# Feed-forward tail: running sums held on the chip, the residual added by the output's DMA, a quarter of two convolutions on ACT and POOL, and the second up weights split earlier

## The chip, the cores and the metric

The kernel runs on one core of a Trainium2 chip. The metric is the device time of one execution in microseconds (us). TensorE (PE) does matmuls, VectorE (DVE), ScalarE (ACT) and GpSimd (POOL) work element by element, and SyncE (SP) and POOL issue DMAs.

## The reference

One block of a diffusion model, depth 1, on 2048 tokens of width 1024, in float32. What matters here is its second half:

```python
h_lat = h_lat + mod_l[2] * rmsnorm(mix_l, g_post_mix[l])          # residual after the token mix
hl = modulate(h_lat, g_pre_ffn[l], mod_l[3], mod_l[4])
z = (hl @ w_up).reshape(1, 32, 64, 5632)                          # up projection, tokens as a 32 x 64 grid
z = depthwise_conv_3x3(z, conv_w) + conv_b
f_l = (gelu(z[..., :2816]) * z[..., 2816:]) @ w_down              # down projection
h_lat = h_lat + mod_l[5] * rmsnorm(f_l, g_post_ffn[l])
```

The first half (normalisation, a recurrent unit, pooling, a gated unit, an output projection) makes `mix_l` and is not touched, apart from where its result is kept.

## The kernel before, in words

Every float32 operand of a large matmul is split into two float16 halves, and each product is three matmuls (high by high, high by low, low by high). `hT` (128 x 2 x 8 x 2048 float16, 64 KB in each partition) holds the split input of the up projection for all tokens.

The feed-forward part goes over 22 chunks `c` of 128 channels, each with a pair `ab` (the gelu side and the product side). For a chunk, `up` (L835) does 8 blocks of 24 matmuls of 128 x 512 into the two "B" banks, and ACT copies each block into `z`. `conv` (L986) does the 3 x 3 convolution of the chunk in two halves `q` of 16 rows and two sides: ACT writes the middle tap into a PSUM tile, and DVE adds the eight others with one instruction each (L1002); then comes gelu, the product (L1010) and a sum of squares for the scale of the split. Two chunks make a group, eleven groups in all. `split_g` (L1014) splits a group's products, and `down` (L1030) multiplies them with the down weights, in 16 tiles `t` of 128 tokens, 12 matmuls each. The 16 sums over groups live in device memory as `accd`: the first group writes them, later ones add to them with an accumulating DMA that POOL issues (L1064, tile `dd`). The last group instead loads `accd` back (L1040), loads the residual `hlat` (L1042), and `finish` (L1067) adds, normalises and writes the output.

The weights of a chunk are loaded and split by `load_up` (L815): a scale from the sum of squares (ACT L151, one small matmul `sct`, DVE), the high half on ACT (L825), a scaled copy on ACT (L827), the low half on POOL (L828). Chunk 0 is prepared while the output projection of the token mix runs (`i == 5` in the loop over its 16 tiles), chunk 1 in the first pass of the chunk loop. That loop (from L1080) lets `up` of chunk c, `conv` of chunk c-1 and `down` of the group before advance by turns; a scheduler with a timeline of its own then sets the order of each engine's instructions, which run in order on the chip. Work on the last group's two halves, and what is left of group 9 (12 of its 16 tiles), comes after the last up projection. That stretch is called the tail.

Of the kernel before, what the change touches and what calls it, by code (L numbers as in the profile page):

```python
# [15 lines left out]
D = 1024  # L16
# [52 lines left out]
def block_kernel(ctx: ExitStack, tc: tile.TileContext, x, xT, ctx_d, ctxT, cc, crow, cols_d, wm01, bm01, wmT,  # L69
# [32 lines left out]

    hlat = dram.tile([L, D], F32, name="hlat")
    ybc = [dram.tile([128, 4, CH], F32, name=f"ybc{n}") for n in range(NCH)]
# [77 lines left out]
    def rawt(name):  # L182
        return wspp.tile([128, 1024], F32, tag="raw", bufs=2, name=name)

# [630 lines left out]
    def load_up(c):  # L815

        r = fwc.tile([128, 2, 1024], F32, tag="ur", bufs=1, name="ur")
        S.dma_start(r, wup[c].rearrange("p a k m -> p a (k m)"))
        w = (fwc if c % 2 == 0 else ff).tile([128, 2, 2, 1024], F16, tag="uw", bufs=1, name="uw")

        def steps():
            stat(w[:, 0].bitcast(BF16), [r], upsc[:, c, :])
            V.tensor_scalar(upinv[:, c:c + 1], upsc[:, c, 1:2], sc_f[:, 1:2], None, op0=OP.mult)
            yield
            A.activation(w[:, 0], r, AF.Copy, scale=upsc[:, c, 0:1])  # L825
            yield
            A.activation(r, r, AF.Copy, scale=upsc[:, c, 0:1])  # L827
            G.tensor_tensor(w[:, 1], r, w[:, 0], op=OP.subtract)  # L828
            yield

        return w.rearrange("p h a (k m) -> p h a k m", k=KT), steps()

# [3 lines left out]
    def up(c, z, w, order=(0, 1, 2, 3)):  # L836
        for b in order:
            for ab in range(2):
                ps = pB("up")
                mm3(ps, lambda k: w[:, 0, ab, k, :], lambda k: w[:, 1, ab, k, :],  # L840
                    lambda k: hT[:, 0, k, b * CH:(b + 1) * CH], lambda k: hT[:, 1, k, b * CH:(b + 1) * CH])
# [4 lines left out]
    yscale = {}  # L846

# [33 lines left out]
    def residual(n, tt, ps, xr):  # L881
# [45 lines left out]
    for i in range(len(tiles) + 2):  # L927
        if i < len(tiles):
            n, tt = tiles[i]
            if tt == 2 and OUT.index(n) + 2 < NCH:  # L930
                y_scale(OUT[OUT.index(n) + 2])
            pr[i] = project(n, tt)
        if i == 5:
            wn, lu = load_up(0)
            list(lu)
        if 0 <= i - 1 < len(tiles):
            residual(*tiles[i - 1], *pr[i - 1])
        if i == len(tiles):
            z0 = zp.tile([128, 2, 32, 64], F32, tag="z", name="z")
            up0 = up(0, z0, wn, OUT)  # L940
# [42 lines left out]

    def conv(c, z, gs, gsq):

        for q in range(2):  # L986
            r0 = q * 16
            cv = []
            for ab in range(2):
                def wt(dy, dx):  # L990
                    return col("fcw", (c + NP * ab) * 9 + (dy + 1) * 3 + dx + 1)
# [39 lines left out]
    def down(gi, q, sp, di):  # L1031
# [35 lines left out]
    def finish(t, a, hr):  # L1067
# [12 lines left out]
    dws, queue = {}, []  # L1080
    dn, cvn, ld = nothing, nothing, nothing
    gs, gsq = None, None
    for c in range(NP + 1):
        gi, i = divmod(c, GRP)
        if c < NP:
            z = (ff if c % 2 else zp).tile([128, 2, 32, 64], F32, tag="z", bufs=1, name="z") if c else z0
            upn, lu = up(c, z, wn) if c else nothing, nothing
            if c + 1 < NP:
                wn, lu = load_up(c + 1)
            if i == 0:  # L1090
                ld = load_down(gi)
        else:
            upn = lu = nothing
        for s in range(8):
            next(upn, None)
            if s > 0:
                next(lu, None)
                if s % 2 == 0:
                    next(ld, None)
            if c != NP - 1:  # L1100
                for _ in range(1 if c < NP else 2):
                    if next(dn, queue) is queue and queue:
                        dn = queue.pop(0)
                        next(dn)
            next(cvn, None)
            if s % 4 == 3 and c > 0 and i == 0:
                q = s // 4
                queue.append(down(gi - 1, q, *split_g(gi - 1, q, gs, gsq)))
        if 2 <= c < 10:
# [4 lines left out]
        if c < NP:  # L1114
            if i == 0:
                gs = [[], []]
                gsq = small.tile([128, 2, GRP], F32, tag="gsq", bufs=2, name="gsq")
            cvn = conv(c, z, gs, [gsq[:, q, i:i + 1] for q in range(2)])
    for d in [dn] + queue:
# [96 lines left out]
```

## Time and profile before

| | us |
|---|---|
| median of 3 runs (2192.57 to 2199.12) | 2194.92 |
| the profiled execution | 2195.05 |
| its span, first to last instruction | 2193.3 |
| PE busy | 2034.2 (93%) |
| DVE busy | 1593.0 (73%) |
| ACT busy | 1192.5 (54%) |
| POOL busy | 603.0 (27%) |

The slices of the page show three stretches in which PE is far from full after the start: around 400 to 560 us (inside the token mix), around 780 us (between chunk 0 and chunk 1 of the feed-forward part), and from about 2095 us to the end. A busy PE is not PE at full speed: the granted clock (PEclk, 1.00 is 2.4 GHz and 0.50 is 1.2 GHz) is to be read with it.

### The profile page before, as it was taken

How to read it: one execution, taken by the hardware profiler on the slowest of the kernel's cores; microseconds unless marked ns; L12 is line 12 of the kernel's file. 1: busy time of each engine (PE TensorE's matmuls, PEld its weight loads, DVE VectorE, ACT ScalarE, POOL GpSimd, SP SyncE). 2: the span in 40 equal slices, each digit the busy share in tenths (PEclk: the TensorE clock that was granted, in tenths of full speed). 3: DMA queues.
4: the chain of work that ended last, by engine and by line, in shares of the span. 5: the costliest groups of instructions: out<-in, count | busy, mean ns of one | idle time of the engine just before them, and what ended most of it. 6: DMA issues, size and time to landing. Idle time of an engine off the chain costs nothing.

```text
span 2193.3 us, 24364 instructions
## 1 busy us (share of the span) xinstructions
PE 2034.2 (93%) x9215; PEld 935.4 (43%) x9215; DVE 1593.0 (73%) x2218; ACT 1192.5 (54%) x1661; POOL 603.0 (27%) x453
## 2 busy tenths in 40 slices
PE   6868989797999979999999999999999999999964
PEld 1433444343455434444444444444444444444421
DVE  5687788999554279867787677668776776778844
ACT  4676755454354456656565555646465555645431
POOL 2232334444255321002121211211122221212144
PEclk8889999898999989999999999999999999999987
DMA  7521153513332110325455554545454454444387
GB/s 292 191 93 60 66 161 110 157 37 104 130 135 100 69 58 29 135 87 108 81 124 88 124 91 83 106 68 105 87 106 87 87 106 87 88 86 87 64 236 256
DMA packets 77514, 239.48 MB, mean 109 GB/s; under 512 B 7890, under 2 KB 18514, under 8 KB 72530
## 3 DMA queue, kind: packets, MB, share of 16 engines
q1 hardware_dynamic: 56660, 162.42, 22.0%
q0 software_dynamic: 20736, 75.51, 21.2%
q8 instruction: 72, 1.18, 0.2%
q14 instruction: 46, 0.38, 0.1%
HBM read 128.84 MB, written 109.05 MB: 108 GB/s over the span
## 4 chain that ended last, share of the span: by engine, by line
PE 69%; DVE 13%; DMA 6%; issue 5%; ACT 5%; POOL 2%; SPq 0%; POOLq 0%; DVEq 0%; ACTq 0%
PE up L359 13%; PE up L361 13%; PE up L360 13%; PE dn L1049 6%; PE dn L1051 6%; PE dn L1050 6%; PE wo L874 3%; PE wo L876 3%; PE wo L878 3%; DVE wm L660 2%; DMA ac<-accd 1%; DMA wm<-in_wmT_dram 1%; DVE lru L479 1%; ACT L136 1%; DMA hT<-in_wm_dram 1%
## 5 line engine op out<-in xcount | busy, mean ns | idle before, releaser
L1002 DVE SCALAR_TENSOR_TENSOR cv<-z,cols,cv 128x1008 f32<-128x1008 f32 (+2 forms) x704 | 871.6, 1251 | 278.7 <-ACT cv L995 186.6
L359 PE MATMUL up<-hT,uw 128*128 128x512 f16 x1408 | 535.3, 380 | 6.2 <-ACT uw L825 3.7
L361 PE MATMUL up<-hT,uw 128*128 128x512 f16 x1408 | 534.7, 380 | 6.3 <-POOL uw L828 6.3
L360 PE MATMUL up<-hT,uw 128*128 128x512 f16 x1408 | 535.1, 380 | 0.0
L1064 POOL DMA_DIRECT2D accd<-dd x144 | 124.6, 865 | 762.4 <-ACT dd L1060 756.3
L842 ACT ACTIVATE z<-up,upinv 128x512 f32<-128x512 f32 x176 | 120.8, 686 | 355.3 <-PE up L361 354.8
L1049 PE MATMUL dn<-dw,gs 128*128 128x512 f16 x704 | 270.8, 385 | 33.3 <-DVE ac L1055 30.4
L1060 ACT ACTIVATE dd<-dn,gdi 128x512 f32<-128x512 f32 x320 | 214.1, 680 | 115.9 <-PE dn L1051 111.2
L1050 PE MATMUL dn<-dw,gs 128*128 128x512 f16 x704 | 271.1, 385 | 0.0
L1051 PE MATMUL dn<-dw,gs 128*128 128x512 f16 x704 | 269.9, 386 | 0.0
L361 PEld LDWEIGHTS <-uw 128*128 128x128 f16 x1408 | 137.9, 98 | 174.1 <-POOL uw L828 7.2
L359 PEld LDWEIGHTS <-uw 128*128 128x128 f16 x1408 | 139.0, 99 | 168.8 <-ACT uw L825 3.8
L360 PEld LDWEIGHTS <-uw 128*128 128x128 f16 x1408 | 138.0, 98 | 168.2 <-issue 4.7
L828 POOL TENSOR_TENSOR uw<-ur,uw 128x2048 f16<-128x2048 f32 x22 | 89.5, 4068 | 196.8 <-ACT ur L827 165.2
L136 ACT ACT_TABLE_LOAD x77 | 98.8, 1283 | 47.9 <-PE rp L443 24.1
L1050 PEld LDWEIGHTS <-gs 128*128 128x128 f16 x704 | 69.5, 99 | 117.7 <-issue 43.3
L1049 PEld LDWEIGHTS <-gs 128*128 128x128 f16 x704 | 72.9, 104 | 81.2 <-issue 4.9
L995 ACT ACTIVATE cv<-z,cols 128x1024 f32<-128x1024 f32 x88 | 106.0, 1205 | 2.0
L1051 PEld LDWEIGHTS <-gs 128*128 128x128 f16 x704 | 69.6, 99 | 85.8 <-issue 4.6
L979 POOL TENSOR_TENSOR dw<-dr,dw 128x1024 f16<-128x1024 f32 x22 | 46.4, 2125 | 117.3 <-PE dn L1051 100.6
L874 PE MATMUL wo<-wo,ysp 128*128 128x512 f16 x256 | 77.2, 383 | 1.1 <-ACT gm L807 1.1
L876 PE MATMUL wo<-wo,ysp 128*128 128x512 f16 x256 | 77.2, 383 | 0.0
(299 smaller groups left out, 3013.5 us busy)
## 6 DMA issues: line engine op xcount, KB each, us to landing
accd<-dd POOLq DMA_DIRECT2D x144, 512.0 KB, 5.3
ur<-in_wup_dram SPq DMA_DIRECT2D x22, 1024.0 KB, 5.6
wm<-in_wmT_dram SPq DMA_DIRECT2D x64, 256.0 KB, 2.9
dr<-in_wdn_dram SPq DMA_DIRECT2D x22, 512.0 KB, 4.4
hT<-in_wm_dram SPq DMA_DIRECT2D x8, 1024.0 KB, 14.5
xt<-in_xT_dram SPq DMA_DIRECT2D x8, 1024.0 KB, 7.0
ro<-in_wout_dram SPq DMA_DIRECT2D x16, 512.0 KB, 4.0
xr<-in_x_dram SPq DMA_DIRECT2D x16, 512.0 KB, 3.5
```

Source lines behind the costliest of these rows:

```text
L359: T.matmul(ps, wh(k), hh(k), start=(k == 0), stop=False)
L360: T.matmul(ps, wh(k), hl(k), start=False, stop=False)
L361: T.matmul(ps, wl(k), hh(k), start=False, stop=(k == KT - 1))
L842: A.activation(z[:, ab, b * 8:(b + 1) * 8, :], ps.rearrange("p (r x) -> p r x", x=64), AF.Identity, scale=upinv[:, c:c + 1])
L874: T.matmul(ps[h], ysp[:, 0, k, :], wk[:, 0, h * CH:(h + 1) * CH], start=st, stop=False)
L876: T.matmul(ps[h], ysp[:, 0, k, :], wk[:, 1, h * CH:(h + 1) * CH], start=False, stop=False)
L1002: V.scalar_tensor_tensor(o, z[:, ab, ya + dy:yb + dy, xa + dx:xb + dx], wt(dy, dx), o, op0=OP.mult, op1=OP.add)
L1049: T.matmul(ps[h], hi, wh, start=i == 0, stop=False)
L1050: T.matmul(ps[h], hi, wl, start=False, stop=False)
L1051: T.matmul(ps[h], lo, wh, start=False, stop=i == n - 1)
L1060: A.activation(d[:, h * CH:(h + 1) * CH], ps[h], AF.Copy, scale=di)
L1064: G.dma_start(accd[t], d, accum_op=OP.add)
```

## The change

Five edits. (1) `load_up(1)` moves from the chunk loop to `i == 9` of the output projection's loop, and the loads of later chunks follow. For odd chunks the split weights go to two tiles of a pool `rwp` that is kept to the end. (2) The residual goes into the output tensor instead of `hlat`, and `finish` adds the normalised sum to it with an accumulating DMA issued by POOL. (3) After the last up projection `hT` is not read any more; the 16 sums are loaded from `accd` into its memory (`acc`), the 12 tiles of group 9 that come in the tail are added there by POOL, and the last group adds to it on DVE. (4) In chunks 20 and 21, the product side of the second half of the convolution is done by ACT (a scaled copy per tap) and POOL (an addition per tap). (5) In the tail, odd tiles use the "B" banks, and in `finish` every fourth tile is scaled on ACT and POOL instead of DVE.

```diff
+            w = [rwp.tile([128, 2, 1024], F16, tag="raw", name=f"uw{e}") for e in range(2)]
...
-        S.dma_start(hlat[tok:tok + 128, :], hl)
+        kept[tok // 128] = S.dma_start(out[tok:tok + 128, :], hl)
...
+        if i == 9:
+            wn, lu = load_up(1)
+            list(lu)
...
+    def conv_pool(c, z, cvp):
+
+        t = fwc.tile([128, 2, 16, 64], F32, tag="uw", bufs=1, name="cvp")
+        cvp.append(t[:, 0])
+        m = fwc.tile([128, 2, 16, 64], F32, tag="ur", bufs=1, name="tap")
+        w = [col("fcw", (c + NP) * 9 + e) for e in range(9)]
+        A.activation(t[:, 0], z[:, 1, 16:32, :], AF.Identity, bias=col("fcb", c + NP), scale=w[4])
+        yield
+        for n, (dy, dx) in enumerate(TAPS):
+            ya, yb, xa, xb = area(16, dy, dx)
+            o, v = (e[:, ya - 16:yb - 16, xa:xb] for e in (t[:, 0], m[:, n % 2] if n % 3 else t[:, 1]))
+            A.activation(v, z[:, 1, ya + dy:yb + dy, xa + dx:xb + dx], AF.Copy, scale=w[(dy + 1) * 3 + dx + 1])
+            G.tensor_tensor(o, o, v, op=OP.add)
+            yield
...
-            if last:
-                a = fa.tile([128, D], F32, tag="dd", bufs=3, name="ac")
-                S.dma_start(a, accd[t])
-                hr = ff.tile([128, D], F32, tag="dr", name="hr")
-                S.dma_start(hr, hlat[t * 128:(t + 1) * 128, :])
-            ps = [pC(f"dn{h}") for h in range(2)]
+            tail = phase["tail"]
+            ps = [(pB if tail and t % 2 else pC)(f"dn{h}") for h in range(2)]
...
-                    b = a[:, h * CH:(h + 1) * CH]
+                    b = acc[:, t, h * CH:(h + 1) * CH]
                     V.scalar_tensor_tensor(b, ps[h], di, b, op0=OP.mult, op1=OP.add)
-                finish(t, a, hr)
+                finish(t, acc[:, t, :])
...
+                elif tail:
+                    G.tensor_tensor(acc[:, t, :], acc[:, t, :], d, op=OP.add)
                 else:
                     G.dma_start(accd[t], d, accum_op=OP.add)
...
+    acc = hT.bitcast(F32).rearrange("p a k t -> p (a k t)").rearrange("p (t d) -> p t d", d=D)
...
-        V.scalar_tensor_tensor(a, a, m[:, 1:2], gm5, op0=OP.mult, op1=OP.mult)
-        G.tensor_tensor(hr, a, hr, op=OP.add)
-        S.dma_start(out[t * 128:(t + 1) * 128, :], hr)
+        if t % 4 == 3:
+            A.activation(a, a, AF.Copy, scale=m[:, 1:2])
+            G.tensor_tensor(a, a, gm5, op=OP.mult)
+        else:
+            V.scalar_tensor_tensor(a, a, m[:, 1:2], gm5, op0=OP.mult, op1=OP.mult)
+        end = G.dma_start(out[t * 128:(t + 1) * 128, :], a, accum_op=OP.add)
...
+            phase["tail"] = True
+            for t in range(NT):
+                S.dma_start(acc[:, t, :], accd[t])
```

The order of the instructions moves at three places that matter. The first is ACT's row at the end of chunk 0's up projection. `uw` and `ur` are split and raw up weights (of chunk 1 before, of chunk 2 now), `dw` and `dr` the same for the down weights, `cv` the middle taps of the first convolution. Before:

```order
L842 ACTIVATE z<-up,upinv 128x512
L151 ACTIVATE uw,stt<-ur 128x2048
L151 ACTIVATE dw,stt<-dr 128x1024 x2
L842 ACTIVATE z<-up,upinv 128x512 x3
L995 ACTIVATE cv_5800<-z,cols 128x1024
L995 ACTIVATE cv_5877<-z,cols 128x1024
L825 ACTIVATE uw<-ur,upsc 128x2048
```

Now:

```order
L846 ACTIVATE z<-up,upinv 128x512
L150 ACTIVATE dw,stt<-dr 128x1024 x2
L846 ACTIVATE z<-up,upinv 128x512 x3
L150 ACTIVATE uw,stt<-ur 128x2048
L1025 ACTIVATE cv_5803<-z,cols 128x1024
L1025 ACTIVATE cv_5880<-z,cols 128x1024
```

The squares of the next weights stood ahead of the last blocks of the up projection; now they stand behind them, right ahead of the convolution's first instructions. The split of chunk 1 (L825 and L827 before) has left this place.

The second is ACT's row after the last eviction of the last up projection (`z`). `dd` is the eviction of a tile of group 9, `cvp` and `tap` are the convolution's sum and scaled copies. Before:

```order
L842 ACTIVATE z<-up,upinv 128x512
L995 ACTIVATE cv_15147<-z,cols 128x1024
L1060 ACTIVATE dd<-dn_14819,gdi 128x512
L1060 ACTIVATE dd<-dn_14820,gdi 128x512
L1060 ACTIVATE dd<-dn_14837,gdi 128x512
L1060 ACTIVATE dd<-dn_14838,gdi 128x512
```

Now:

```order
L846 ACTIVATE z<-up,upinv 128x512
L1000 ACTIVATE cvp<-z,cols 128x1024
L1005 ACTIVATE cvp<-z,cols 128x16x63
L1005 ACTIVATE tap<-z,cols 128x1024
L1005 ACTIVATE tap<-z,cols 128x16x63
L1085 ACTIVATE dd<-dn_14875,gdi 128x512
L1085 ACTIVATE dd<-dn_14904,gdi 128x512
L1085 ACTIVATE dd<-dn_14905,gdi 128x512
L1085 ACTIVATE dd<-dn_14876,gdi 128x512
L1005 ACTIVATE cvp<-z,cols 128x16x63
```

The middle tap and three scaled copies now stand ahead of the first evictions.

The third is POOL's row in the tail: before, one issue of an accumulating DMA for each tile of group 9, then `finish` of the last group (the power that gives the normaliser, `fms`, and the residual's addition, `hr`).

```order
L1064 DMA accd_5731<-dd 128x1024
L1064 DMA accd_5732<-dd 128x1024
L1064 DMA accd_5733<-dd 128x1024
L160 TENSOR_TENSOR fms<-rst,mhalf 128x1
L1073 TENSOR_TENSOR hr<-ac,hr 128x1024
```

Now the additions of group 9 (L1089) and the eight of chunk 21's convolution (L1006, the first of them the first row here) take turns, and the output's DMAs come behind them:

```order
L1006 TENSOR_TENSOR cvp<-cvp 128x16x63
L1006 TENSOR_TENSOR cvp<-cvp,tap 128x1024
L1089 TENSOR_TENSOR hT<-hT,dd 128x1024
L1006 TENSOR_TENSOR cvp<-cvp,tap 128x16x63
L1089 TENSOR_TENSOR hT<-hT,dd 128x1024 x2
...
L1089 TENSOR_TENSOR hT<-hT,dd 128x1024
L159 TENSOR_TENSOR fms<-rst,mhalf 128x1 x2
L1006 TENSOR_TENSOR cvp<-cvp,tap 128x15x63
L159 TENSOR_TENSOR fms<-rst,mhalf 128x1
L1107 DMA out_dram<-hT 128x1024 x3
```

Twelve tile additions and eight taps have come onto POOL ahead of the first output DMA; the twelve accumulating issues of group 9 and the sixteen residual additions have gone.

## Rows read from the trace of the kernel before

**Rows 1.** Stretches: busy us (instructions) of each engine, granted clock, DMA share, GB/s.

```profile
750.00:800.00 50.00, 39.24 (x170) 17.37 (x168) 21.92 (x27) 26.35 (x34) 10.56 (x5) 0.83 0.21 69
800.00:850.00 50.00, 48.68 (x229) 22.41 (x227) 48.55 (x50) 25.32 (x31) 4.07 (x1) 1.00 0.06 21
...
1950.00:2000.00 50.00, 50.00 (x238) 23.18 (x236) 37.73 (x43) 29.53 (x36) 8.94 (x7) 1.00 0.41 64
...
2100.00:2150.00 50.00, 33.53 (x121) 13.35 (x121) 30.20 (x46) 14.73 (x24) 25.98 (x18) 0.84 0.75 255
```

**Rows 2.** Timeline, ACT and POOL, second weights: start, us, instruction, idle before.

```profile
761.67 1.90 ACT L151 ACTIVATE uw<-ur 128x2048 bf16<-128x2048 f32 x1
...
776.62 0.69 ACT L842 ACTIVATE z<-up,upinv 128x512 f32<-128x512 f32 x1 [4.49 <-PE up L361]
...
797.71 0.69 ACT L842 ACTIVATE z<-up,upinv 128x512 f32<-128x512 f32 x1 [0.20 <-PE up L361]
...
785.71 4.07 POOL L828 TENSOR_TENSOR uw<-ur,uw 128x2048 f16<-128x2048 f32 x1 [24.27 <-ACT ur L827]
```

**Rows 3.** Timeline of DVE and PE, first convolutions to the first split.

```profile
778.59 18.59 DVE L1002 SCALAR_TENSOR_TENSOR cv<-z,cols,cv 128x945 f32<-128x945 f32 x16
...
843.77 0.15 DVE L1018 TENSOR_REDUCE gt<-gsq 128x1 f32<-128x2 f32 x1
...
855.93 0.28 PE L122 MATMUL sct<-gt,ones 128*128 128x1 f32 x2
```

**Rows 4.** Waits of the tail: engine, line, what it waited for, us, times, longest.

```profile
DVE ac L1055 <- DMA ac<-accd: 48.6, 13, 20.5
```

**Rows 5.** The chain of waits at the tail's first load: start, us, what.

```profile
2093.37 6.86 DMA ac<-accd
```

**Rows 6.** Timeline of ACT and POOL, tail: last up block, group 9 tile.

```profile
2059.62 0.69 ACT L842 ACTIVATE z<-up,upinv 128x512 f32<-128x512 f32 x1 [1.80 <-PE up L361]
...
2090.21 0.86 POOL L1064 DMA_DIRECT2D accd<-dd  x1 [1.73 <-ACT dd L1060]
```

**Rows 7.** A stretch of 5 us behind the wait for that load.

```profile
2100.00:2105.00 5.00, 3.74 (x9) 1.32 (x9) 2.55 (x5) 1.15 (x2) 0.56 (x1) 0.50 0.41 143
```

**Rows 8.** Groups of instructions in the tail: count, busy us, mean ns, idle before.

```profile
L1055 DVE SCALAR_TENSOR_TENSOR ac<-dn,gdi,ac 128x512 f32<-128x512 f32 x32 | 22.7, 746 | 51.0 <-DMA ac<-accd 48.6 <-PE dn L1051 2.5
L1072 DVE SCALAR_TENSOR_TENSOR ac<-ac,fms,gm 128x1024 f32<-128x1024 f32 x16 | 20.4, 1276 | 3.3 <-POOL fms L160 3.3
...
L1070 ACT ACTIVATE fo<-ac 128x1024 bf16<-128x1024 f32 x16 | 16.9, 1057 | 68.5 <-DVE ac L1055 60.6 <-POOL hr L1073 3.5 <-DVE scq L127 2.9
L1060 ACT ACTIVATE dd<-dn,gdi 128x512 f32<-128x512 f32 x24 | 16.3, 685 | 12.0 <-PE dn L1051 8.9 <-DMA accd<-dd 3.0
...
L995 ACT ACTIVATE cv<-z,cols 128x1024 f32<-128x1024 f32 x2 | 2.4, 1207 | 0.1
...
L1073 POOL TENSOR_TENSOR hr<-ac,hr 128x1024 f32<-128x1024 f32 x16 | 37.5, 2342 | 38.9 <-DVE ac L1072 24.4 <-DVE rst L159 8.3 <-DMA hr<-hlat 3.9
L160 POOL TENSOR_TENSOR fms<-rst,mhalf 128x1 f32<-128x1 f32 x16 | 9.8, 611 | 10.1 <-DVE rst L159 10.1
```

**Rows 9.** Groups on POOL from 600 us on: DMA issues, the first residual's addition.

```profile
L1064 POOL DMA_DIRECT2D accd<-dd x144 | 124.6, 865 | 762.4 <-ACT dd L1060 756.3 <-ACT junk L151 6.1
...
L896 POOL TENSOR_TENSOR hl<-hl,xr 128x1024 f32<-128x1024 f32 x13 | 35.0, 2694 | 23.7 <-DVE hl L894 23.7
```

**Rows 10.** DMA under group 9's last sums: packets, MB, share; issues.

```profile
q0 software_dynamic: 1582, 5.79, 101.0%
...
accd<-dd POOLq DMA_DIRECT2D x12, 512.0 KB, 5.6
```

**Rows 11.** DMA queues over the whole span: packets, MB, share.

```profile
q0 software_dynamic: 20736, 75.51, 21.2%
```

**Rows 12.** Timeline of POOL and DVE where the two meet in the tail.

```profile
2120.93 2.35 POOL L1073 TENSOR_TENSOR hr<-ac,hr 128x1024 f32<-128x1024 f32 x1 [2.25 <-DVE gsc L128]
...
2122.13 2.23 DVE L1027 SCALAR_TENSOR_TENSOR gs<-g,gsc,gs 128x1024 f16<-128x1024 f32 x1 [0.91 <-ACT gs L1026]
```

More of the change, by code (lines that the diff above doesn't have):

```diff
@@ L101, in block_kernel @@
     open_psum("ps0", 4, 2, 2)
-    hlat = dram.tile([L, D], F32, name="hlat")
     ybc = [dram.tile([128, 4, CH], F32, name=f"ybc{n}") for n in range(NCH)]
@@ L182, in rawt @@
     def rawt(name):
-        return wspp.tile([128, 1024], F32, tag="raw", bufs=2, name=name)
+        return rwp.tile([128, 1024], F32, tag="raw", name=name)
     xts = {}
@@ L818, in load_up @@
         S.dma_start(r, wup[c].rearrange("p a k m -> p a (k m)"))
-        w = (fwc if c % 2 == 0 else ff).tile([128, 2, 2, 1024], F16, tag="uw", bufs=1, name="uw")
+        if c % 2:
+            w = [rwp.tile([128, 2, 1024], F16, tag="raw", name=f"uw{e}") for e in range(2)]
+        else:
+            w = fwc.tile([128, 2, 2, 1024], F16, tag="uw", bufs=1, name="uw")
+            w = [w[:, e] for e in range(2)]
         def steps():
-            stat(w[:, 0].bitcast(BF16), [r], upsc[:, c, :])
+            stat(w[0].bitcast(BF16), [r], upsc[:, c, :])
             V.tensor_scalar(upinv[:, c:c + 1], upsc[:, c, 1:2], sc_f[:, 1:2], None, op0=OP.mult)
             yield
-            A.activation(w[:, 0], r, AF.Copy, scale=upsc[:, c, 0:1])
+            A.activation(w[0], r, AF.Copy, scale=upsc[:, c, 0:1])
             yield
             A.activation(r, r, AF.Copy, scale=upsc[:, c, 0:1])
-            G.tensor_tensor(w[:, 1], r, w[:, 0], op=OP.subtract)
+            G.tensor_tensor(w[1], r, w[0], op=OP.subtract)
             yield
-        return w.rearrange("p h a (k m) -> p h a k m", k=KT), steps()
+        return [e.rearrange("p a (k m) -> p a k m", k=KT) for e in w], steps()
     gm2 = row_of("gm2", on_, 0, col("gqm", 0, 8))
@@ L844, in up @@
                 yield
-    yscale = {}
+    yscale, kept = {}, {}
     def y_scale(n):
@@ L982, in block_kernel, with area, conv @@
     TAPS = [(dy, dx) for dy in (-1, 0, 1) for dx in (-1, 0, 1) if (dy, dx) != (0, 0)]
-    def conv(c, z, gs, gsq):
+    def area(r0, dy, dx):
+        return max(r0, -dy), min(r0 + 16, 32 - dy), max(0, -dx), min(64, 64 - dx)
+    def conv_pool(c, z, cvp):
[11 more added lines that the diff above has]
+            yield
+    def conv(c, z, gs, gsq, cvp=None):
         for q in range(2):
@@ L989, in conv @@
             for ab in range(2):
+                if cvp is not None and (q, ab) == (1, 1):
+                    cv.append(cvp[0].rearrange("p r x -> p (r x)"))
+                    yield
+                    continue
                 def wt(dy, dx):
@@ L1080, in block_kernel @@
     dws, queue = {}, []
-    dn, cvn, ld = nothing, nothing, nothing
+    phase = {"tail": False}
+    dn, cvn, ld, cvq = nothing, nothing, nothing, nothing
     gs, gsq = None, None
     for c in range(NP + 1):
-        gi, i = divmod(c, GRP)
         if c < NP:
+            gi, i = divmod(c, GRP)
             z = (ff if c % 2 else zp).tile([128, 2, 32, 64], F32, tag="z", bufs=1, name="z") if c else z0
             upn, lu = up(c, z, wn) if c else nothing, nothing
-            if c + 1 < NP:
+            if 0 < c < NP - 1:
                 wn, lu = load_up(c + 1)
@@ L1099, in block_kernel @@
                     next(ld, None)
[L1100 to L1104, printed above, removed]
+            for _ in range(1 if c < NP - 1 else 2 * (c == NP)):
+                if next(dn, queue) is queue and queue:
+                    dn = queue.pop(0)
+                    next(dn)
+            next(cvq, None)
+            next(cvq, None)
             next(cvn, None)
-            if s % 4 == 3 and c > 0 and i == 0:
+            if s % 4 == 3 and c > 0 and c % GRP == 0:
                 q = s // 4
-                queue.append(down(gi - 1, q, *split_g(gi - 1, q, gs, gsq)))
+                queue.append(down(c // GRP - 1, q, *split_g(c // GRP - 1, q, gs, gsq)))
         if 2 <= c < 10:
@@ L1117, in block_kernel @@
                 gsq = small.tile([128, 2, GRP], F32, tag="gsq", bufs=2, name="gsq")
-            cvn = conv(c, z, gs, [gsq[:, q, i:i + 1] for q in range(2)])
+            cvp = [] if c >= NP - 2 else None
+            cvn = conv(c, z, gs, [gsq[:, q, i:i + 1] for q in range(2)], cvp)
+            if cvp is not None:
+                cvq = conv_pool(c, z, cvp)
     for d in [dn] + queue:
```

15 lines of the change are left out of this document (9 added, 6 removed).

## The prediction

> **What bounds the kernel now.** I read the stretches of 50 us first, with the granted clock beside them. From 950 us to the tail PE is busy 50.00 of 50 us at clock 1.00, with DVE at 37.73 [rows 1]. There nothing but fewer matmuls helps, and the change takes none away. Two places are different. Between 750 and 800 us PE has 39.24 us at 0.83, and in 2100 to 2150 us it has 33.53 us at 0.84 while DMA is at 0.75 [rows 1]. The timeline shows what each is.
>
> The first is the wait for chunk 1's weights. ACT evicts chunk 0's last block at 776.62 and the next block, chunk 1's first, at 797.71 [rows 2]; blocks otherwise follow in 0.69 + 4.49 = 5.18 us (the first of these two rows: its time and the idle before). So 797.71 - 776.62 - 5.18 = 15.9 us are lost. POOL's half of the split starts only at 785.71 and takes 4.07 [rows 2].
>
> The second is the tail. The last up block is evicted from 2059.62 on. Group 9's tiles then pass at 0.86 + 1.73 = 2.59 us each, the pace of PE [rows 6]. The first load of a sum starts at 2093.37 and takes 6.86 [rows 5]; DVE waits for such loads 48.6 us in all [rows 4]. Loads, residual loads and output writes share the DMA engines, and 16 tiles take from there to the end of the span, 2193.3: 100 us.
>
> **First part: the second weights.** Everything between up(0) and up(1) on PE goes away, so PE starts chunk 1 some 15.9 us sooner. The work moves into the output projection: 1.90 us of squares and two scaled copies of about that length on ACT, 4.07 on POOL [rows 2], a small matmul. PE sets the pace there and these engines have gaps. If their cover were gone it would cost at most the 10 us they sum to.
>
> But DVE does not start sooner: its first convolution waits for chunk 0's last block, as before, and runs without a gap (18.59 us for 16, [rows 3]; 48.55 of 50 busy, [rows 1]). The order now even puts the squares of chunk 2's weights, 1.90 + 0.2, ahead of its first middle tap on ACT (0.2 us, here and below, is the reading of an accumulated sum; steps of one column are put at 0.15). DVE reaches the sum that scales the first split at 843.77 [rows 3], so now at about 845.9. PE's small matmul on it stands at 855.93 [rows 3] and would come at 840.0. It waits 5.9 us, and 10.0 of the 15.9 are left. Behind it DVE is faster than PE for each chunk (37.73 to 50, [rows 1]), so it catches up and the 10 us stay. Bounds: 15.9 if DVE finds no such wait, 4 if the second half of the group waits as well. I take 10.
>
> **Second part: the tail.** Times are those of the trace of before, the 10 us not yet taken off. One of the 12 tiles of group 9 now stands among the last up blocks on PE, so the last eviction starts 2.6 us later, at 2062.2.
>
> *Loads.* The 16 loads start when the last up block has read its last row of `hT`, about 2057.5. No accumulating DMA runs beside them. At 255 GB/s [rows 1] one takes 2.06 us, so the seventh, which POOL needs first (tile 4), is there at about 2074.
>
> *POOL.* After the eviction (0.69) ACT does the middle tap and the first scaled copy, 1.21 each [rows 8], so POOL starts at 2065.3. Twenty additions stand there: 12 tiles and 8 taps. None like them in that place is in the trace; the nearest row is the residual's addition of the same shape, 2.342 [rows 8], the far one the same addition beside a busier DVE, 2.694 [rows 9]. Not less than 2.342: no row of this shape is shorter. I take 2.34: 46.8 us. With two powers (0.61 each, [rows 8]) and some 4 us of wait for tile 4's load after the first two taps, the last tap is added at 2117.3. Before, POOL had 12 issues of 0.865 here [rows 9]. PE, ACT and the three `dd` buffers wait for POOL: group 9 is held to POOL's pace, and the last group's first tiles start at about 2100, as before, when the first load was there (2093.37 + 6.86, [rows 5]). So that wait is exchanged, not removed.
>
> *Second half of the last group.* DVE's product waits for the last tap: 2117.3 + 1.28 (as L1072, [rows 8]), the squares 1.06 + 0.19, 1.5 for the sum, the small matmul and the scale, 1.14 for the split's high half: 2122.5. By then seven of 16 tiles are through at 2.59 each, and PE has waited some 4 us. Nine tiles are left: 9 x 2.59 = 23.3, and 2.6 more because PE restarts at the lower clock after a wait (0.50 in 2100 to 2105, [rows 7]). DVE keeps up: 2 x 0.746 + 1.276 + 0.15 = 2.92 for three tiles in four, 1.64 for the fourth, 2.60 on average. That is 2148.4. The last tile then takes 0.75 + 1.25 + 0.15 + 0.61 on DVE, ACT, DVE and POOL, 1.14 + 2.34 for the scaling on ACT and POOL, and 5.6 for its DMA [rows 8, 10]: 2160.2.
>
> *Output DMAs.* They must be issued by POOL, so the first comes behind the last tap, at about 2118. In the trace 12 such DMAs at one per 2.59 us keep the engines at 101.0% [rows 10]. Sixteen: 2118 + 16 x 2.59 + 3 (5.6 of the last, less its own 2.6) = 2162.5. This ends last, barely. Bounds: the queue's share of the whole span gives 0.212 x 2193.3 / 144 = 3.23 us each [rows 9, 11], and then the end is 2172.7; the other end is no queue at all, 2160.2. I take 2.59, measured where they were as dense.
>
> So the tail ends at 2162 instead of 2193.3: 31 us.
>
> *At nothing:* the residual's write to the output (the same DMA as to `hlat`); chunk 20's taps, 9 x 1.21 on ACT and 8 x 2.34 on POOL, in a pass where both have half their time free (ACT 29.53, POOL 8.94 of 50, [rows 1]). The product of chunk 20 then comes some 4 us later on DVE, which holds chunk 21's convolution back as much; DVE has 10 us of work less behind it. Without that cover, 4 us.
>
> **The sum.** 2195.05 (profiled execution) - 10 - 31 = 2154 us. That execution and the median, 2194.92, are the same within 0.01%.
>
> **Where POOL and DVE meet.** While POOL's addition ran from 2120.93 for 2.35 us, DVE's split, of the size of L1072 with its 1.276 [rows 8], began at 2122.13 and took 2.23: it ended some 1.1 us after POOL's end [rows 12]. So such pairs do not overlap, and in the tail each costs up to one DVE instruction. About five DVE instructions of this kind fall into POOL's chain (two split halves, three normalisations): 5 x 1.27 = 6 us, an end near 2169 at worst. The Trainium skill says this in "SBUF — State Buffer", section "Who interferes with whom": a DVE instruction with two SBUF inputs and a GpSimd instruction that reads SBUF block each other for the whole instruction. The trace agrees, with the 2.23 us. The convolution's instructions have one input in PSUM and would be free of it by that page, so the long part of the chain would not be touched.
>
> **Rivals.**
> - *The heavier tail or no gain in front.* DMAs at 3.23 us (end 2172.7), additions at 2.69 (24 x 0.35 = 8 us), the meetings above (6 us), or DVE taking back all of the first part: each leaves about 2164. For it: POOL gets some 80 us of work in a tail of 100. Against: the measured 2.59.
> - *PE bounds the tail.* If additions and taps keep out of each other's way, 27 tiles x 2.59 from 2062.2 end at 2132.1, and with 12 us for the last tile at 2144: 2195 - 10 - 49 = 2136. Against: twenty additions in one queue alone need 46.8 us of those 70.
> - *Slower: PE at half clock.* Each wait for POOL's additions leaves PE idle, and if the clock stays at 0.50, as after the wait of 6.9 us [rows 7], a tile takes 5.18 us. 27 x 5.18 = 140, so 2062.2 + 140 + 11.8 = 2214 and 2195 + 21 - 10 = 2206. It decides from about 4.9 us per tile on, where the tail's end is 10 us later than before. Against it: 2100 to 2150 us, with longer waits, still had 0.84 on average [rows 1]. By the Trainium skill ("TensorE: Matmul & The Clock Gate", section "What's actually happening") the lower level is the default and activity releases it; the rows show both levels.
>
> **How the numbers follow.** 0.60 for my sum (own range 2148 to 2160), 0.20 for 2164, 0.15 for 2136, 0.03 for the half clock, 0.02 for something that leaves no change. The range 2138 to 2175 takes in the bounds of DMA and additions and most of the faster case. 0.3%, 6.6 us, is about what a measurement of this kernel can tell. Faster 0.95, the same 0.02, slower 0.03.
>
> **What would show it.** Chunk 1's first block evicted about 5 us after chunk 0's last; the small matmul on the first sum waiting some 6 us for DVE. In the tail no wait for `accd` on DVE beyond the start; POOL nearly without idle time from the first tap to the last, about 52 us; the first output DMA some 55 us after the last up block; then DMA near 1.0 to the end. I am wrong if POOL has gaps there, if additions differ much from 2.34, or if the output DMAs come at another pace than 2.6.

## The result and the profile after

The changed kernel takes 2170.61 us (median of 4 runs, 2168.78 to 2172.35), the kernel before, timed beside it, 2194.61 (2192.57 to 2199.12): a ratio of 0.9888, 95% interval 0.987 to 0.9906. The forecast was 2154, with a range of 2138 to 2175. It was faster, as forecast, but by 24 us and not by 41. The profiled execution took 2169.70 us, its span 2167.5.

To compare executions I cut each into three stretches at two instructions that every version has: POOL's first addition of a residual in the output projection, and one of DVE's sums `gt` (two for each group, 22 in all), the one at 1720.17 before. It is the sixteenth, the second half of the eighth group; the expectations below call it the sum of the last but one group, which it is not. From it to the same sum two groups on (1970.18 before, 1964.76 after) it is 250.0 us in both kernels, so the stretch behind it holds that much unchanged loop ahead of the tail proper. In the changed kernel the two instructions stand here (timeline of POOL and of DVE: start, duration, instruction, idle time before it and what ended it):

```profile
572.39 2.35 POOL L900 TENSOR_TENSOR hl<-hl,xr 128x1024 f32<-128x1024 f32 x1 [1.91 <-DVE hl L898]
...
1714.76 0.16 DVE L1047 TENSOR_REDUCE gt<-gsq 128x1 f32<-128x2 f32 x1 [0.72 <-ACT junk L150]
```

| us | before | after | forecast of the gain | gain |
|---|---|---|---|---|
| start to the first residual addition (not touched by the change) | 571.37 | 572.39 | 0 | -1.0 |
| from there to the sum: front | 1148.80 | 1142.37 | 10 | 6.4 |
| from the sum to the end of the span: tail | 473.13 | 452.74 | 31 | 20.4 |

The first stretch lies between 570.5 and 579.6 in the fourteen executions profiled here, whatever was edited behind it. A change of a few microseconds is therefore read from the two other stretches, and the medians only confirm it. Where versions share the code of a front it agrees within 0.7 us, and a shared tail within 1.6 (one profile of each), so a smaller difference shows nothing.

The same stretches as in [rows 1], after (the busy time of PE, PEld, DVE, ACT and POOL with their instructions, the granted clock, the DMA share, GB/s):

```profile
750.00:800.00 50.00, 48.56 (x231) 22.64 (x230) 19.75 (x25) 23.93 (x32) 10.39 (x5) 1.00 0.13 48
800.00:850.00 50.00, 43.84 (x202) 20.07 (x201) 49.61 (x50) 26.26 (x32) 5.50 (x2) 0.95 0.12 42
1950.00:2000.00 50.00, 50.00 (x238) 23.18 (x236) 34.75 (x41) 30.16 (x38) 13.41 (x9) 1.00 0.34 54
2100.00:2150.00 50.00, 39.17 (x166) 16.88 (x164) 39.83 (x62) 22.93 (x37) 37.23 (x34) 0.89 0.66 115
```

The hole before chunk 1 (39.24 at 0.83) is gone, and a smaller one stands 50 us later. The middle is unchanged, the tail better filled. The two waits of PE that matter, and one behind the second (timeline of PE):

```profile
848.50 0.59 PE L121 MATMUL sct<-gt,ones 128*128 128x1 f32 x2 [5.50 <-DVE gt L1047]
...
2115.40 0.59 PE L121 MATMUL sct<-gt,ones 128*128 128x1 f32 x2 [5.92 <-DVE gt L1047]
2128.29 0.38 PE L1074 MATMUL dn<-dw,gs 128*128 128x512 f16 x1 [1.59 <-DVE hT L1080]
...
2146.30 0.38 PE L1076 MATMUL dn<-dw,gs 128*128 128x512 f16 x1
```

The first is what [rows 3] has become, the second is the wait for the last tap, and the last row is the last matmul. After both waits PE works at the lower level of the granted clock (1.2 GHz), as in [rows 7]: for 3.4 us behind the first and 6.4 us behind the second, in which a matmul's row shows up to 0.63 us and not 0.38 (windows):

```profile
845.00:850.00 5.00, 1.50 (x5) 0.86 (x6) 4.97 (x7) 2.25 (x3) 0.92 (x1) 0.52 0.61 210
850.00:855.00 5.00, 5.00 (x20) 2.05 (x19) 5.00 (x8) 2.75 (x3) 0.00 (x0) 0.80 0.01 3
...
2115.00:2120.00 5.00, 4.60 (x12) 1.92 (x13) 3.64 (x11) 3.88 (x5) 2.87 (x5) 0.50 1.04 196
2120.00:2125.00 5.00, 5.00 (x20) 2.08 (x19) 4.12 (x3) 0.79 (x1) 3.24 (x2) 0.82 1.07 194
```

POOL in the tail, first tap, last tap, first output DMA, last scaling and last output DMA (timeline of POOL), and then the group of its tile additions:

```profile
2059.92 2.34 POOL L1006 TENSOR_TENSOR cvp<-cvp 128x1008 f32<-128x1008 f32 x1 [26.18 <-ACT cvp L1005]
...
2107.60 2.88 POOL L1006 TENSOR_TENSOR cvp<-cvp,tap 128x945 f32<-128x945 f32 x1
2110.45 1.53 POOL L159 TENSOR_TENSOR fms<-rst,mhalf 128x1 f32<-128x1 f32 x1
2111.93 1.78 POOL L1107 DMA_DIRECT2D out_dram<-hT  x2
...
2153.92 2.66 POOL L1104 TENSOR_TENSOR hT<-hT,gm 128x1024 f32<-128x1024 f32 x1
2156.88 0.87 POOL L1107 DMA_DIRECT2D out_dram<-hT  x1 [0.30 <-POOL hT L1104]
```

```profile
L1089 POOL TENSOR_TENSOR hT<-hT,dd 128x1024 f32<-128x1024 f32 x12 | 30.0, 2521 | 1.0 <-DMA hT<-accd 1.0
```

The wait of [rows 4, 5] for the sums is down to 1.0 us on POOL. The last eviction of an up block ([rows 6] before) now starts here (timeline of ACT):

```profile
2056.79 0.69 ACT L846 ACTIVATE z<-up,upinv 128x512 f32<-128x512 f32 x1
```

DVE's last sum of the down projection ends at 2147.7, the span 19.8 us behind it. The output DMAs hold the engines like this from the first issue to 3.6 us before the end, in a thin stretch and in a dense one of it (windows):

```profile
2111.90:2163.90 52.00, 29.69 (x122) 12.77 (x122) 33.76 (x53) 20.74 (x32) 32.49 (x34) 0.76 0.91 161
2126.00:2140.00 14.00, 12.41 (x59) 5.51 (x57) 12.15 (x20) 5.82 (x11) 8.98 (x11) 1.00 0.65 101
2142.00:2163.00 21.00, 4.68 (x22) 1.85 (x19) 8.60 (x15) 7.03 (x12) 13.41 (x13) 0.67 1.06 197
```

The share 0.91 of 52.00 us is 47.3 us of busy time, 2.96 for each of 16 DMAs. That is not the time that one takes in a row of them: the share goes above 1 where they are dense, so the times of packets overlap in this count. By the bytes, 197 GB/s in the dense stretch, 512 KB take 2.66 us. Sixteen take 42.6 of the 52.0 us, and 9.4 are gaps, the time from the first issue to the first packets among them.

### The profile page after: what moved, and what is told of

The parts are those of the page before. It is cut to its first block, busy times and chain, and to the rows that moved or that the text cites. A ratio compares the mean times of both kernels' runs of the same rounds, so it can differ in the third digit from the quotient of the medians.

```text
span 2167.5 us, 24301 instructions
## 1 busy us (share of the span) xinstructions
PE 2027.0 (94%) x9215; PEld 933.8 (43%) x9215; DVE 1579.6 (73%) x2198; ACT 1211.3 (56%) x1681; POOL 649.3 (30%) x473
## 4 chain that ended last, share of the span: by engine, by line
PE 54%; DVE 3%; POOL 2%; issue 1%; DMA 1%; ACT 1%; POOLq 0%; SPq 0%; DVEq 0%; ACTq 0%
PE up L359 12%; PE up L360 12%; PE up L361 12%; PE dn L1074 6%; PE dn L1076 6%; PE dn L1075 6%; DVE cv L1031 2%; POOL hT L1089 1%; DMA hT<-accd 1%; DVE hT L1106 1%; POOL cvp L1006 0%; DVE hT L1080 0%; POOL hT L1104 0%; DMA wm<-in_wmT_dram 0%; POOL fms L159 0%
## 5 line engine op out<-in xcount | busy, mean ns | idle before, releaser
L1031 DVE SCALAR_TENSOR_TENSOR cv<-z,cols,cv 128x1008 f32<-128x1008 f32 (+3 forms) x688 | 851.2, 1250 | 271.2 <-ACT cv L1025 183.3
L1091 POOL DMA_DIRECT2D accd<-dd x132 | 114.3, 866 | 696.8 <-ACT dd L1085 690.7
L1074 PE MATMUL dn<-dw,gs 128*128 128x512 f16 x704 | 267.9, 380 | 12.1 <-ACT dd L1085 10.5
L1075 PE MATMUL dn<-dw,gs 128*128 128x512 f16 x704 | 267.9, 381 | 0.0
L1076 PE MATMUL dn<-dw,gs 128*128 128x512 f16 x704 | 265.8, 380 | 0.0
L150 ACT ACTIVATE junk<-g 128x1024 bf16<-128x1024 f32 x44 | 46.3, 1053 | 63.3 <-DVE g L1039 63.1
L878 PE MATMUL wo<-wo,ysp 128*128 128x512 f16 x256 | 77.5, 384 | 1.0 <-ACT gm L807 1.0
```

The lines of the kernel that those rows point to most:

```text
L1074: T.matmul(ps[h], hi, wh, start=i == 0, stop=False)
L1075: T.matmul(ps[h], hi, wl, start=False, stop=False)
L1076: T.matmul(ps[h], lo, wh, start=False, stop=i == n - 1)
```

## The experiments

Each was timed beside the kernel before. Ratio and interval are to that kernel; the two stretches are those of the table above (tail: from the sum to the end of the span).

| kernel | median us | ratio (95%) | front us | tail us |
|---|---|---|---|---|
| changed kernel | 2170.61 | 0.9888 (0.987 to 0.9906) | 1142.37 | 452.74 |
| late_w2 | 2178.34 | 0.9926 (0.9902 to 0.995) | 1148.66 | 454.23 |
| plain_out | 2167.03 | 0.9861 (0.984 to 0.9882) | 1141.90 | 445.43 |
| gm_dve | 2167.21 | 0.9874 (0.9851 to 0.9896) | 1141.92 | 448.86 |
| plain_gm | 2162.82 | 0.9842 (0.9826 to 0.9859) | 1142.00 | 442.61 |
| last_dve | 2168.80 | 0.9862 (0.9848 to 0.9875) | 1142.49 | 451.91 |
| dve_adds | 2163.63 | 0.9844 (0.9829 to 0.986) | 1142.18 | 445.67 |
| conv_dve | 2156.11 | 0.9812 (0.9794 to 0.983) | 1142.49 | 437.43 |
| conv_20 | 2154.38 | 0.9795 (0.978 to 0.9809) | 1142.56 | 437.49 |
| best | 2151.49 | 0.9789 (0.9773 to 0.9804) | 1141.80 | 435.94 |
| best2 | 2150.01 | 0.9783 (0.9767 to 0.9799) | 1141.72 | 433.92 |
| front_hold | 2171.67 | 0.987 (0.9857 to 0.9884) | 1138.55 | 454.32 |
| best3 | 2141.49 | 0.9729 (0.9716 to 0.9743) | 1134.96 | 430.83 |

**What the first part is worth.** late_w2:

```diff
-        if i == 9:
-            wn, lu = load_up(1)
-            list(lu)
...
-            if 0 < c < NP - 1:
+            if c < NP - 1:
                 wn, lu = load_up(c + 1)
```

> Chunk 1's up weights are split where they were before, behind chunk 0's up blocks; the tail stays as changed. Theory, the earlier split is worth what the first sums show: the time rises by 5 to 6 us, to about 2176. The forecast had said 10. Rival, DVE falls behind there in either order and the gain is taken back by the tail's start: no change within 1.5 us.

The front is 1148.66, that of before within 0.2: the whole gain of the front is this edit, 6.3 us, and the tail does not take it back. The time rose by more than the 5 to 6 us expected (ratio 0.9926 to 0.9888), with wide intervals. In the output projection the moved steps cost nothing: from the first residual addition to the last it is 165.48 us with them and 165.30 without.

**What the output DMAs are worth.** plain_out leaves the residual out of the result:

```diff
-        end = G.dma_start(out[...], a, accum_op=OP.add)
+        end = G.dma_start(out[...], a)
```

> The output DMAs write the scaled tile only and do not add to what stands in the output; so the residual is left out of the result. Theory, the last nine DMAs queue at about 2.6 us each behind POOL's late issue: plain writes take about half of that, so the last one lands 3 to 4 us after its issue instead of 9 to 10, and the time falls by 5 to 7 us, to about 2164 to 2166. Rival, the chain of POOL and DVE up to the last issue sets the end and a DMA's own latency is the rest: less than 2 us.

The tail is 7.3 us shorter. The medians show less, 2167.03, since the first stretch of this kernel's profile is 578.37. The window over its output DMAs, and the view of its DMA issues (count, KB, median time to landing):

```profile
2116.40:2164.00 47.60, 28.47 (x122) 12.53 (x122) 33.82 (x53) 20.73 (x32) 28.09 (x34) 0.83 0.43 177
```

```profile
out_dram<-hT POOLq DMA_DIRECT2D x16, 512.0 KB, 3.0
```

0.43 of 47.60 us is 1.28 us of busy time for one, against 2.96 by the same count, and in the changed kernel the landing takes 7.4:

```profile
out_dram<-hT POOLq DMA_DIRECT2D x16, 512.0 KB, 7.4
```

So the theory holds in the main. The last DMA landed 4.9 us after its issue (2165.7 - 2160.26 - 0.58), against 9.8 in the changed kernel and 3 to 4 expected, and the median of 2164 to 2166 was just missed.

**What POOL's share of the scaling is worth.** gm_dve replaces `if t % 4 == 3` by `if False`, last_dve by `if t % 4 == 1`:

> All sixteen tiles are scaled by DVE, none over ACT and POOL. Theory of the forecast, POOL's additions of 2.3 us and DVE's instructions on the same memory do not overlap: with the four POOL instructions gone, DVE's longest scalings in the second half (2.5 us and more) come back to 1.28, which pays for the four that it takes over; the end comes 1 to 3 us sooner, as the last tile's chain is shorter as well. Rival, DVE paces the second half (2 x 0.75 + 1.28 and two small steps a tile is more than PE's 2.59): its work grows by 5 us and the time rises by 1 to 4 us.

> The tiles whose scaling goes over ACT and POOL are 1, 5, 9, 13 instead of 3, 7, 11, 15, so the last tile is scaled by DVE. Theory, the end behind the last product (9 us to the last issue, 10 more to its landing) is partly the last tile's own chain: one DVE instruction of 1.28 replaces 1.15 on ACT and 2.6 on POOL with POOL's waiting issues between, so the time falls by 2 to 4 us. Rival, the output DMAs queue at 2.6 us each and it is their queue that ends: less than 1 us.

All on DVE the tail is 3.9 us shorter, more than the 1 to 3 expected: DVE's own work did not decide. From the small matmul on the last sum to the end of the last matmul PE takes 29.1 us instead of 31.3. In the changed kernel the last split of the second half stood beside POOL's scaling of a tile, and in gm_dve it does not (timeline of DVE, changed kernel and gm_dve):

```profile
2120.57 2.89 DVE L1056 SCALAR_TENSOR_TENSOR gs<-g,gsc,gs 128x1024 f16<-128x1024 f32 x1
```

```profile
2122.01 1.27 DVE L1056 SCALAR_TENSOR_TENSOR gs<-g,gsc,gs 128x1024 f16<-128x1024 f32 x1
```

Moving POOL's share to other tiles gives 0.8, which is within the spread and below the 2 to 4 expected: now a scaling of DVE stood beside POOL's at the end and took 3.36 instead of 1.28. plain_gm leaves the residual out too and makes both edits:

> Both at once: the output DMAs write without adding (the residual is left out of the result) and all tiles are scaled by DVE. Measured from the sum of the last but one group of DVE (at 1714.76 in the changed kernel's trace) to the end of the span, the changed kernel takes 452.7 us, plain writes alone 445.4, DVE's scaling alone 448.9. Theory, the shortfall behind the last product has two parts in series, POOL's scaling chain and the queue of accumulating DMAs: about 441 to 443 us. Rival, both remove the same wait: 445 or more.

442.61: the two add up (452.7 - 7.3 - 3.9 = 441.5). That the forecast's tail was 473.1 - 31 = 442.1 is a coincidence: it had accumulating DMAs and POOL's scalings in it. With one DVE instruction for the last tile's scaling (1.28 for 1.14 + 2.34) and a plain landing (3.0 for 5.6) its own chain would have ended at 435.3, and plain_gm still takes 7.3 more. The last matmul ends there as forecast, 86.3 us behind the last up eviction; the last issue follows after 8.4 us and not 4.0, and the end after 5.9 and not 3.0.

**What the convolution on POOL is worth.** conv_dve sets `cvp = None`; conv_20 gives POOL chunk 20 but not 21; dve_adds keeps both and lets DVE add group 9's tiles straight from PSUM:

```diff
-            cvp = [] if c >= NP - 2 else None
+            cvp = [] if c == NP - 2 else None      # conv_20
...
+            elif tail:                             # dve_adds
+                for h in range(2):
+                    b = acc[:, t, h * CH:(h + 1) * CH]
+                    V.scalar_tensor_tensor(b, ps[h], di, b, op0=OP.mult, op1=OP.add)
```

> The quarter of the convolution of the last two chunks goes back from ACT and POOL to DVE (eight instructions of about 1.25 us in each chunk). Theory, POOL's queue of twenty additions sets the tail: with twelve left, group 9 passes at the pace of PE and the last output DMAs are issued some 12 to 18 us sooner; DVE's convolution ends 10 to 20 us later than now but still ahead of PE's second half. The time falls by 10 to 17 us, to about 2154 to 2161. Rival, DVE was the late engine there and the move to POOL is what made the tail short: the time rises by 5 us or more.

> Only chunk 20 gives a quarter of its convolution to ACT and POOL; chunk 21's stays on DVE. Theory, what costs is POOL's eight taps for chunk 21 among its twelve tile additions: without them the last output DMA is issued some 10 us sooner, as in the run with the whole convolution on DVE, and chunk 20's taps cost nothing or help a little, since DVE then reaches chunk 21 some 10 us sooner: 2152 to 2158 us. Rival, chunk 20's taps are what hurts, by delaying its product on DVE by 4 us or more: at or above 2165.

> Group 9's twelve tail tiles are added to their sums by DVE straight from PSUM (two instructions of about 0.75 us a tile) and no longer by ACT's two evictions and POOL's 2.5 us. Theory, POOL's queue of twenty additions sets the tail: POOL then has only the eight taps, done about 20 us after the last up block instead of 53; PE goes through its 27 tiles at 2.59 us and the output DMAs start some 15 us sooner, so the time falls by 14 to 20 us, to about 2150 to 2157. Rival, DVE paces the second half anyway: it gets 18 us more work and the time falls by 4 us or less. Second rival, the pace of the output DMAs alone: they still come in one row of 16 x 2.6 us from about the same first issue, and the time falls by less than 4 us.

Both conv runs came out as expected: without chunk 21's taps on POOL the tail is 15.3 us shorter, and chunk 20's taps are free (437.43 and 437.49). POOL's twelve additions then run behind each other, the first output DMA goes 40 us behind the last up block and not 55, and PE has six short waits in the whole tail, the longest of 1.13 us (timelines of POOL and of PE of conv_20):

```profile
2067.98 27.47 POOL L1089 TENSOR_TENSOR hT<-hT,dd 128x1024 f32<-128x1024 f32 x11 [0.21 <-DMA hT<-accd]
...
2097.60 0.89 POOL L1107 DMA_DIRECT2D out_dram<-hT  x1 [1.62 <-DVE rst L158]
```

```profile
2068.54 0.38 PE L1074 MATMUL dn<-dw,gs 128*128 128x512 f16 x1 [0.57 <-ACT dd L1085]
...
2101.83 0.38 PE L1074 MATMUL dn<-dw,gs 128*128 128x512 f16 x1 [1.13 <-DVE hT L1080]
```

dve_adds gained 7.1 in the tail and missed its 14 to 20. Its taps were done at 2080, but DVE was in the last convolution until 2068 and PE waited 6.03 us for its first tiles at 2066.95. That the queue of twenty is what costs holds; taking the tiles out of it is the worse half to take.

**Why PE waits for the first sum.** best holds ACT's squares of chunk 2's weights behind two middle taps and lets this chunk's weights begin two up blocks later (with conv_20 and all scaling on DVE in the tail). front_hold is one edit to the changed kernel:

```diff
+                    if c == 1 and q == 1:
+                        hold(tap, [runs["prod"]])
...
+            runs["prod"] = V.tensor_tensor(g, g, cv[1], op=OP.mult)
```

> Chunk 21's convolution back on DVE, all scaling on DVE, and in the front ACT's squares of chunk 2's weights held behind the first two middle taps of chunk 0's convolution. Theory of the front: DVE's first convolution then starts about 2 us sooner, PE's wait for the first sum falls from 5.5 to about 3.5, and the stretch from the first residual addition on POOL to the sum of the last but one group is 1140 to 1141 us instead of 1142.4; rival, the wait comes from elsewhere and it stays. Theory of the tail: 437.5 with chunk 21's convolution on DVE, less 2 to 4 for the scaling: 434 to 436 us from that sum to the end. Rival: with ten us more work DVE paces the second half and the stretch stays at 437 or grows. Together 2147 to 2152 us against 2154 to 2156.

> One edit to the changed kernel: on DVE the taps of chunk 1's second half stand behind the product of its first half, so 50 convolution instructions stand ahead of the first group's first sum, as before the change, instead of 53. Theory, the 5.5 us that PE waits for this sum are made of those three instructions (3.6 us) and ACT's squares: the sum comes some 3.5 us sooner, PE's wait falls to about 2, the lower clock after it shrinks or goes, and the stretch from the first residual addition on POOL to the sum of the last but one group falls from 1142.4 to 1137 to 1139 us; time 3 to 5 us less, about 2166. Rival, DVE is late by its whole work and not by the order: the wait is only moved to the next sum and the stretch stays within 1 us.

In the tail best reached the expected 434 to 436 with 435.94 us, though the 1.6 below conv_20 are no more than the spread. It missed in the front: the first convolution starts 1.75 us sooner, the sum at the same place. The number of convolution instructions ahead of this sum on DVE says why (the group of that line from the first one to the sum; before, changed, best, front_hold):

```profile
L1002 DVE SCALAR_TENSOR_TENSOR cv<-z,cols,cv 128x1008 f32<-128x1008 f32 (+3 forms) x50 | 59.1, 1249 | 0.6 <-ACT cv L995 0.4
```

```profile
L1031 DVE SCALAR_TENSOR_TENSOR cv<-z,cols,cv 128x1008 f32<-128x1008 f32 (+3 forms) x53 | 62.9, 1249 | 2.3 <-ACT cv L1025 2.1
```

```profile
L1031 DVE SCALAR_TENSOR_TENSOR cv<-z,cols,cv 128x1008 f32<-128x1008 f32 (+3 forms) x54 | 64.0, 1250 | 0.5 <-ACT cv L1025 0.3
```

```profile
L1031 DVE SCALAR_TENSOR_TENSOR cv<-z,cols,cv 128x1008 f32<-128x1008 f32 (+3 forms) x50 | 59.7, 1250 | 2.4 <-ACT cv L1025 2.1
```

Three more stand there after the change, four more in best, which ate its gain. Held back, the wait is 2.47 us, the clock stays at 1.00 behind it, and the front is 3.8 us shorter; the 3 to 5 us expected of the time do not show in the median, 2171.67 (ratio 0.987 against 0.9888, the intervals overlap), and the tail of its profile is 1.6 longer. In PE's timeline of front_hold:

```profile
852.71 0.38 PE L121 MATMUL sct<-gt,ones 128*128 128x1 f32 x2 [2.47 <-DVE gt L1049]
```

**Versions that beat both kernels.** best2 adds a load of the last four tiles' residual into free weight buffers, an addition on POOL (DVE for the last) and a plain write; best3 puts these additions on DVE and has both holds of the front.

```diff
+        if t in hrs:
+            V.tensor_tensor(a, a, hrs[t], op=OP.add)      # best2: POOL, but for t == 15
+            S.dma_start(out[t * 128:(t + 1) * 128, :], a)
+            return
...
+                    hrs[t] = hr[:, e]
+                    ld_ = S.dma_start(hrs[t], out[t * 128:(t + 1) * 128, :])
```

> As the run before, and the residual of the last four tiles is loaded ahead into memory that the weights have left free; POOL (DVE for the very last) adds it, and a plain write takes these four to the output. Theory, behind the last product stands a queue of accumulating DMAs at 2.6 us each: the last write then lands about 3 us after its issue instead of 9 or more, and the stretch from the sum of the last but one group to the end is 5 to 7 us shorter than in the run before. Rival, POOL's four additions and DVE's scalings hold each other up and give most of it back: less than 2 us.

> The run with the residual loaded ahead for four tiles, with that residual added by DVE and not by POOL, and with the same hold in the front. Theory of the tail, POOL's additions and DVE's scalings held each other up there (5.76 us for three scalings, 3.25 for the last addition): the stretch from the sum of the last but one group to the end falls from 433.9 to 430 to 432. Rival, DVE is the late engine at the end and four more instructions cost it what the wait had cost: 433.5 or more. Front: as in the other run, 1137 to 1139. Together 2144 to 2148 us.

In best2 most of the gain was given back (2.0 us are left of 5 to 7, at the bound that its rival named): DVE's last scalings and POOL's additions held each other up. Timeline of DVE, of best2 and then of best3:

```profile
2139.82 5.76 DVE L1102 SCALAR_TENSOR_TENSOR hT<-hT,fms,gm 128x1024 f32<-128x1024 f32 x3
2145.61 3.25 DVE L1104 TENSOR_TENSOR hT<-hT,hr 128x1024 f32<-128x1024 f32 x1
```

```profile
2127.89 2.49 DVE L1104 SCALAR_TENSOR_TENSOR hT<-hT,fms,gm 128x1024 f32<-128x1024 f32 x2
2130.28 0.17 DVE L158 TENSOR_SCALAR rst<-fms 128x1 f32<-128x1 f32 x1
2130.34 2.37 DVE L1106 TENSOR_TENSOR hT<-hT,hr 128x1024 f32<-128x1024 f32 x2
...
2134.47 1.23 DVE L1106 TENSOR_TENSOR hT<-hT,hr 128x1024 f32<-128x1024 f32 x1
```

On DVE alone they take 1.2 us each, and the tail is 430.8. With both holds, 49 convolution instructions stand ahead of the first sum and PE does not wait for it; the front is 1135.0, 13.8 us below before, more than the forecast's 10 and than the 1137 to 1139 expected of this run. The tail is in its range of 430 to 432. best3 takes 2141.49 us (2139.01 to 2142.57), a little less than the 2144 to 2148 expected, a ratio of 0.9729 (0.9716 to 0.9743) to the kernel before.

## Why the prediction was right, and where it was not

- **Right: the two places, and the order of the tail.** The moved split hides in the output projection. The small matmul waits 5.50 us (forecast 5.9). POOL has 52 us forecast from first to last tap and took 50.6, with 49.5 of them busy; the first output DMA was forecast 55.8 us behind the last up eviction and came after 55.1; the second half's split was forecast after 60.3 and was there after about 60.8. Chunk 20's taps cost nothing. POOL's 52 came out by two misses that cancel: the tile additions took 2.52 us each and not 2.34, and the wait for a load 1.0 and not 4.
- **Front, 10 forecast, 6.4 measured.** PE would have reached the first sum 13.95 us sooner, not 15.9 (848.50 - 5.50 - 572.39 against 855.93 - 571.37): the 15.9 took in a wait of 0.78 for ACT that both kernels have. DVE came 3.5 us later, not 2.1: 1.9 for the squares, as said, and 3.7 for three convolution instructions that now stand ahead of the sum, less 2.2 of waits that went. So 8.45 were left at the sum. About two more went behind it, not told apart: the lower clock after the wait, which the forecast counted in the tail but not here, and a wait of 1.07 that followed. front_hold and best3 show that the order on DVE, not its load, is the cause.
- **Tail, 31 forecast, 20.4 measured: the output DMAs did not run without a gap.** The forecast let them do so from the first issue on, "Sixteen: 2118 + 16 x 2.59 + 3", 44.4 us to the end. It was 55.6. The price of one was nearly right, 2.66 us where they are dense and 42.6 for sixteen (2.59 is the spacing of the last issues of the twelve in the kernel before; on average they stood 2.69 apart). What the forecast had put at nothing are 9.4 us of gaps; 3.6 more stand behind the last packet. The 11.2 too few, less 0.7 by which the first one came sooner, are the shortfall of 10.6. Five DMAs went in the first 11 us, two in the next 15, while POOL waited for the second half's tiles, and nine in the last 19, so the queue was full at the end and the last tile's DMA, priced at 5.6 us, landed 9.8 behind its issue (2167.5 - 2156.88 - 0.87).
- **The same along the engines.** The forecast's other sum, the last tile's chain to 2160.2, was short as well. The last matmul ended 89.9 us behind the last up eviction and not 86.2 (2148.4 - 2062.2), the last issue came 10.2 us behind it and not 6.2, and the end 10.6 behind that and not 5.6. So part of the shortfall lies ahead of the DMAs, in tiles that came late. plain_out takes 7.3 of the shortfall away, gm_dve 3.9; that both together meet it is the coincidence told above.
- **The meeting of POOL and DVE**, put beside the sum as a heavier case of 6 us, was real and belongs into the sum: gm_dve gains 3.9 us, in which a shorter chain of the last tile is contained. It is visible where group 9's pace breaks, on DVE and POOL:

```profile
2056.96 8.95 DVE L1031 SCALAR_TENSOR_TENSOR cv<-z,cols,cv 128x1024 f32<-128x1024 f32 x7
2083.21 0.22 DVE L126 TENSOR_SCALAR scq<-sct,sh 128x1 int32<-128x1 int32 x1 [17.31 <-PE sct L121]
...
2084.84 5.96 DVE L1056 SCALAR_TENSOR_TENSOR gs<-g,gsc,gs 128x1024 f16<-128x1024 f32 x2 [0.91 <-ACT gs L1055]
```

```profile
2084.10 2.33 POOL L1006 TENSOR_TENSOR cvp<-cvp,tap 128x1008 f32<-128x1008 f32 x1
2086.39 6.62 POOL L1089 TENSOR_TENSOR hT<-hT,dd 128x1024 f32<-128x1024 f32 x2
```

Two splits of 1.28 took 5.96, two additions of 2.34 took 6.62. The convolution's seven, with one input in PSUM, kept their 1.28 beside POOL's taps. The Trainium skill ("SBUF — State Buffer", section "Who interferes with whom") says that a DVE instruction with two SBUF inputs contends with a GpSimd instruction that reads SBUF, and that one with at most one SBUF input does not, outside DVE's two-port modes; the rows agree, with 5.96 and 6.62 on the one side and 1.28 on the other.
- **The chances, and luck.** 2170.6 lies outside the range of the sum (2148 to 2160, at 0.60) and inside the wide one. The nearest case is the heavier tail (0.20, "about 2164"), which names the DMAs and the meetings, and the time is 6.6 us above it. That the wide range held is in part luck: it was drawn to take in DMAs at 3.23 us each, a price that no dense stretch here shows, and gaps of that size stood in its place. Of the signs named for being wrong, one came: the output DMAs were issued 3.0 us apart on average and not 2.6. The rival in which additions and taps keep out of each other's way ("PE bounds the tail", 2136) is what best3 comes near to once chunk 21's taps are off POOL: its tail would be 424 us, that of best3 is 430.8.

What stays open: why the stretch before 570 us, which no edit touches, differs by up to 9 us between executions; how much of the 3.7 us by which the last matmul came later than forecast is the lower clock and how much the meetings (in gm_dve, with the same 5.9 us wait, it came 86.6 us behind the last up eviction); and what the sums in `hT` and the odd tiles' "B" banks are worth by themselves, which no run shows.

## What to carry to other kernels

A queue that drains at the end is priced from its first issue, with the gaps in which its producer has nothing, and not as if it were dense from there on. Before work moves to an engine that also issues the last transfers, add up that engine's queue up to the first of them: here eight additions of 2.3 us cost 15 us of the tail, and DVE, which could have done this work, stood idle for 17.3 us meanwhile. And count what stands ahead of a waited-for instruction in the new order, not only how much work its engine has.

## What the runs showed of the hardware

One behind the other, accumulating DMAs of 512 KB to device memory took 2.66 us each (197 GB/s); in this queue they landed 7.4 us after their issue (median), plain writes of the same size after 3.0. By busy time of the 16 DMA engines the two are 2.96 and 1.28 us. Two DVE instructions with two SBUF inputs, 1.28 us each by themselves, took 5.96 us beside POOL's additions; seven with one input in PSUM kept their 1.28. PE worked at the lower level of its granted clock after waits of 5.50 and 5.92 us, and stayed at 1.00 after one of 2.47.
